# A decoder layer's embedding norm: the weights of the norm spread over the partitions by TensorE, two constant products, and scaling in halves

## The chip, the cores and the metric

The kernel runs on one core of a Trainium2 chip. The metric is the device time in microseconds (us) of one execution; lower is better. Engines are named as in the profile: PE is TensorE (matmul), PEld its weight loads, DVE VectorE, ACT ScalarE, POOL GpSimd, SP SyncE. DMAs are issued from the queues of SP, ACT and POOL. L442 is line 442 of the kernel before.

## The reference, cut to what matters

The reference is one inference step of a hybrid decoder layer (differential attention and gated DeltaNet side by side, then a gated ConvFFN) for a prompt of 512 tokens and 8 sample groups of 8 tokens, with 16 learned meta tokens. The change lies in the layer's first step, which normalises the input and multiplies it with the input projection:

```python
def rmsnorm(x, w):
    xf = x.astype(jnp.float32)
    y = xf * lax.rsqrt(jnp.mean(xf * xf, axis=-1, keepdims=True) + RMS_EPS)
    return (y * w.astype(jnp.float32)).astype(x.dtype)
...
    xn = rmsnorm(x, p['ln_mix_pre'])
    h = xn @ p['w_in']
```

`x` has 512 + 64 + 16 rows of 1024, `ln_mix_pre` is one row of 1024 weights, and `w_in` is 1024 x 5640, all float32.

## The kernel before, in words

`embed` loads the input as five tiles `x` of up to 128 tokens (on partitions) by 1024 channels: four of the prompt, one of 80 rows with the sample and meta tokens. It also loads the first two weight tiles of `w_in` (128 columns each, as two chunks `wraw` of 256 KB) and the norm's weights `lnb`. Every token needs the same 1024 weights, so `lnb` is a tile of 128 x 1024 whose partitions all hold the same row: one DMA on SP's queue, issued between tiles 0 and 1, reads the row 128 times (L428).

`norm(i)` scales tile i. ACT squares the tile and sums each row into `ss` (L439); `rsqrt` makes r from it, with a step on DVE (L374) and a power on POOL (L375); DVE then writes `xs` = x times r times `lnb` (L442), 1024 elements in one instruction. `xs` is a ring of three buffers.

`put(i)` transposes the scaled tile on PE, in two groups of four blocks of 128 x 128 (L411), each group into one PSUM bank `ps_t` (a ring of three). Each group is split into two float32r parts: ACT casts it to `xhi`, and DVE subtracts that from the original to get `xlo` (both in `split`, L305 and L306). Weights are split in the same way into `whi` and `wlo`; for the first weight tile POOL does the subtraction, for the others DVE.

`product(i)` multiplies weight tile i with the columns of tiles 0 and 1: 24 matmuls (hi by hi, hi by lo, lo by hi for eight blocks of 128 channels, L263) into a bank `ps_d`, a ring of two, from which ACT copies the result (`qT`, L1112). The columns of tiles 2 to 4 are multiplied after the embedding. All later projections use the same `xhi` and `xlo`.

Within `embed` each of PE, ACT, DVE and POOL runs its instructions in the order in which the code lists them (`manual_schedule`). That order is: norm 0, norm 1, put 0, the first weights' split, put 1, norm 2, product 0, norm 3, the second weights' split, put 2, norm 4, product 1, put 3, put 4. DMAs on SP's queue keep their own order; each waits for one of eight semaphores to come free, and a load of weights also for a buffer (three `wraw`). After the embedding, instructions of all engines are ordered by a scheduler.

Of the kernel before, what the change touches and what calls it, by code (L numbers as in the profile page):

```python
# [13 lines left out]
ALU = mybir.AluOpType  # L14
# [3 lines left out]
D = 1024  # L18
# [131 lines left out]
class Body:  # L150
# [263 lines left out]
    def embed(self, pool):  # L414
        nc, a = self.nc, self.a
        lnb = self.t(pool, [128, D], "lnb", bufs=1)
        xs = []
        for i in range(5):
            rows = 128 if i < 4 else NTL
            x = self.t(pool, [128, D], "x", bufs=5)  # L420
            if i < 4:
                nc.sync.dma_start(x, a["x_prompt"][0, 128 * i : 128 * i + 128])
            else:
                nc.sync.dma_start(x[0:64], a["x_sample"].rearrange("b t d -> (b t) d"))
                nc.sync.dma_start(x[64:66], a["meta_tokens"][14:16])
                nc.sync.dma_start(x[66:80], a["meta_tokens"][0:14])
            if i == 0:
                nc.sync.dma_start(lnb, a["ln_mix_pre"][0].partition_broadcast(128))  # L428
            xs.append((x, rows))
            if i == 1:  # L430
                raws = [self.raw_w(a["w_in"][0], C_Q)]
        raws.append(self.raw_w(a["w_in"][0], C_Q + 128))

        def norm(i):
            x, rows = xs[i]
            y[i] = self.t(pool, [128, D], "xs", bufs=3)
            junk = self.t(pool, [128, D], "junk", bufs=1)
            ss = self.t(self.small, [128, 1], "ss", bufs=4)
            nc.scalar.activation(junk[:rows], x[:rows], AF.Square, accum_out=ss[:rows])  # L439
            r = self.t(self.small, [128, 1], "r", bufs=4)  # L440
            self.rsqrt(r[:rows], ss[:rows], 1.0 / D, EPS, rows, 1)
            nc.vector.scalar_tensor_tensor(  # L442
                out=y[i][:rows], in0=x[:rows], scalar=r[:rows], in1=lnb[:rows], op0=ALU.mult, op1=ALU.mult
            )

        engines = {mybir.EngineType.PE, mybir.EngineType.Activation, mybir.EngineType.DVE, mybir.EngineType.Pool}
        y, w, first = {}, [], []

        def put(i):
            rows = xs[i][1]  # L450
            self.to_transposed(y[i], rows, *self.part(self.x, (128 * i, 128 * i + rows)))

        def product(i):
            first.append((w[i], self.dense(w[i], self.x, HALF_Q[:1])))

        with self.tc.manual_schedule(engines=engines):
            norm(0)
            norm(1)
            put(0)
            w.append(self.split_w(raws[0], eng=nc.gpsimd))  # L460
            put(1)
            norm(2)
            product(0)
            norm(3)
            w.append(self.split_w(raws[1]))
            put(2)
            norm(4)
            product(1)
            put(3)
            put(4)  # L470
        return first
# [1337 lines left out]
```

## Time and profile before

| what | value |
|---|---|
| median of 3 runs | 1219.9 us (1218.33 to 1222.36) |
| the profiled execution | 1219.77 us, its span 1218.0 us |
| granted TensorE clock, mean | 0.991 |
| PE busy | 1159.3 us, 95% |
| DVE, ACT, POOL busy | 638.2, 447.3 and 206.5 us |
| PE busy from 0 to 25 us | 13.81 us |
| PE busy from 30 to 60 us | 30.00 us |

A row of the timeline gives start and duration in us, engine, line, operation, the tile written and the tile read, shapes, and how many instructions it merges; in brackets stand the engine's idle time before it and what ended it. A row of the chain of waits gives start, duration, engine, tile and line. A row of the DMA answer gives destination and source, queue, count, KB of each, and the median us from issue to landing.

### The profile page before, as it was taken

The page shows a single profiled execution, that of the slowest core. Times are in us where ns is not written, and L with a number is a line of the kernel's source. Part 1 is how long each engine was busy: PE and PEld are TensorE (multiplying, and loading weights), DVE is VectorE, ACT ScalarE, POOL GpSimd, SP SyncE. Part 2 cuts the span into 40 slices and gives each one's busy share as a digit, 9 for nine tenths or more (in the row PEclk, how much of TensorE's full clock was granted, in tenths as well). Part 3 has the DMA queues.
Part 4 walks back from the last instruction along what each step waited for, and adds up shares of the span by engine and source line. Part 5 has one row for each costly group of instructions (what it writes and reads, how often), then busy time and mean ns, then how long its engine had stood idle before and what let it go on. Part 6 is the DMA issues. An engine that isn't in the chain of part 4 may idle for free.

```text
span 1218.0 us, 23729 instructions
## 1 busy us (share of the span) xinstructions
PE 1159.3 (95%) x8927; PEld 1036.0 (85%) x8927; DVE 638.2 (52%) x1719; ACT 447.3 (37%) x1139; POOL 206.5 (17%) x341
## 2 busy tenths in 40 slices
PE   6999999979999989899999999999999999999996
PEld 5977787757687677599998987899999999999996
DVE  5456667596487388346235753455545545422224
ACT  5234445443343243343233433433333333323322
POOL 2122221150241231221010002321111111100000
PEclk9999999999999999999999999999999999999999
DMA  6364525736936946713221552322223223352222
GB/s 197 77 237 133 160 64 180 238 113 201 302 108 192 300 154 192 252 47 86 69 70 55 149 163 87 102 81 85 75 86 88 84 75 88 95 166 79 79 80 85
DMA packets 185002, 157.57 MB, mean 129 GB/s; under 512 B 13234, under 2 KB 147315, under 8 KB 184867
## 3 DMA queue, kind: packets, MB, share of 16 engines
q1 hardware_dynamic: 179569, 147.53, 40.1%
q0 software_dynamic: 4288, 5.16, 1.5%
q10 hardware_dynamic: 1030, 3.35, 0.9%
q8 instruction: 71, 1.16, 0.4%
q14 instruction: 44, 0.36, 0.1%
HBM read 146.12 MB, written 9.88 MB: 128 GB/s over the span
## 4 chain that ended last, share of the span: by engine, by line
PE 69%; issue 13%; DVE 9%; POOL 3%; ACT 3%; DMA 2%; SPq 0%; DVEq 0%; ACTq 0%; POOLq 0%
PE ps_d L263 28%; PE ps_g L263 14%; PE ps_t L263 11%; PE ps_s L263 9%; PE ps_t L411 6%; DVE cy L639 1%; PE ps_m L263 1%; DVE KT L1393 1%; DMA page<-in_cache_k 1%; DMA page<-in_cache_v 1%; DVE vt L646 1%; DVE wlo L306 0%; DVE yn L1744 0%; POOL xr L406 0%; ACT whi L305 0%
## 5 line engine op out<-in xcount | busy, mean ns | idle before, releaser
L306 DVE TENSOR_TENSOR wlo<-wraw,whi 128x512 fp32r<-128x512 f32 x238 | 159.6, 684 | 243.6 <-ACT whi L305 241.9
L305 ACT CAST whi<-wraw 128x512 fp32r<-128x512 f32 x240 | 142.7, 613 | 253.9 <-PE ps_d L263 106.6
L263 PE MATMUL ps_d<-xhi,whi 128*128 128x256 f32 (+2 forms) x704 | 219.0, 311 | 0.0
L263 PE MATMUL ps_d<-xhi,wlo 128*128 128x256 f32 (+2 forms) x704 | 213.5, 304 | 1.2 <-DVE wlo L306 1.2
L263 PE MATMUL ps_d<-xlo,whi 128*128 128x256 f32 (+2 forms) x704 | 213.3, 303 | 0.3 <-DVE xlo L306 0.2
L263 PEld LDWEIGHTS ps_d<-xhi,whi 128*128 128x128 f32 x704 | 134.3, 191 | 7.4 <-issue 4.2
L263 PEld LDWEIGHTS ps_d<-xlo,whi 128*128 128x128 f32 x704 | 134.1, 190 | 3.6 <-issue 2.5
L263 PEld LDWEIGHTS ps_d<-xhi,wlo 128*128 128x128 f32 x704 | 133.8, 190 | 2.6 <-DVE wlo L306 1.6
L411 PE MATMUL ps_t<-consts,page 128*128 128x128 f32 x512 | 73.5, 283 | 8.9 <-DVE KT L1393 7.5
L411 PEld LDWEIGHTS ps_t<-consts,page 128*128 128x128 f32 x512 | 57.5, 143 | 25.5 <-issue 10.3
L263 PE MATMUL ps_t<-fhi,whi 128*128 128x320 f32 (+2 forms) x208 | 62.1, 299 | 0.1
L1393 ACT COPY KT<-ps_t 128x512 f32<-128x512 f32 x64 | 37.4, 585 | 65.5 <-PE ps_t L411 62.8
L263 PE MATMUL ps_t<-flo,whi 128*128 128x320 f32 (+2 forms) x208 | 61.3, 295 | 0.0
L263 PE MATMUL ps_t<-fhi,wlo 128*128 128x320 f32 (+2 forms) x208 | 61.1, 295 | 0.0
L263 PE MATMUL ps_g<-fhi,whi 128*128 128x320 f32 (+2 forms) x200 | 59.5, 298 | 0.0
L263 PE MATMUL ps_g<-flo,whi 128*128 128x320 f32 (+2 forms) x200 | 58.9, 295 | 0.0
L263 PE MATMUL ps_g<-fhi,wlo 128*128 128x320 f32 (+2 forms) x200 | 58.7, 294 | 0.0
L263 PE MATMUL ps_d<-fhi,whi 128*128 128x320 f32 (+2 forms) x192 | 57.4, 299 | 0.2 <-ACT fhi L305 0.2
L263 PE MATMUL ps_d<-flo,whi 128*128 128x320 f32 (+2 forms) x192 | 56.8, 296 | 0.0
L263 PE MATMUL ps_d<-fhi,wlo 128*128 128x320 f32 (+2 forms) x192 | 56.7, 296 | 0.0
L1393 DVE COPY KT<-ps_t 128x512 f32<-128x512 f32 x64 | 43.7, 685 | 18.1 <-PE ps_t L411 17.9
L263 PEld LDWEIGHTS ps_t<-fhi,whi 128*128 128x128 f32 x208 | 39.1, 188 | 0.7 <-ACT whi L305 0.3
(554 smaller groups left out, 2824.6 us busy)
## 6 DMA issues: line engine op xcount, KB each, us to landing
page<-in_cache_k SPq DMA_DIRECT2D x128, 256.0 KB, 4.1
page<-in_cache_v SPq DMA_DIRECT2D x128, 256.0 KB, 4.3
wraw<-in_w_in SPq DMA_DIRECT2D x88, 256.0 KB, 3.4
wraw<-in_w_ffn_in SPq DMA_DIRECT2D x88, 256.0 KB, 3.1
wraw<-in_w_down SPq DMA_DIRECT2D x40, 256.0 KB, 3.0
wraw<-in_w_out SPq DMA_DIRECT2D x16, 256.0 KB, 3.0
x<-in_x_prompt SPq DMA_DIRECT2D x4, 512.0 KB, 7.4
st<-in_state_gdn SPq DMA_DIRECT2D x4, 512.0 KB, 4.1
```

The costliest lines, as they stand in the source:

```text
L263: self.nc.tensor.matmul(out, lhsT, rhs, **kw)
L305: self.nc.scalar.copy(hi, raw)
L306: (eng or self.nc.vector).tensor_tensor(out=lo, in0=raw, in1=hi.bitcast(F32), op=ALU.subtract)
L411: self.nc.tensor.transpose(out, in_, self.ident[:k, :k])
L639: nc.vector.scalar_tensor_tensor(out=y, in0=pre[:, j : j + n], scalar=self.cw[:, ch, 24 + j : 25 + j], in1=y, op0=ALU.mult, op1=ALU.add)
L646: nc.vector.scalar_tensor_tensor(out=dst, in0=part(th), scalar=1.0, in1=part(y_), op0=ALU.add, op1=ALU.mult)
L1393: (nc.scalar.copy if j % 2 else nc.vector.tensor_copy)(kt[:, :, 128 * j : 128 * j + 128], tp)
```

## The change

Three things, all in `embed`:

- The weights come as one row of 4 KB (`lnrow`, one partition), by a DMA on ACT's queue behind the 64 KB of the identity. TensorE multiplies a column of 128 ones with each half of that row, which leaves the weights on all 128 partitions of two PSUM banks (`ps_d`, called `lnp` in the code). Norms 0 and 1 read them there. Two ACT copies then fill `lnb` in SBUF for norms 2 to 4. The broadcast DMA on SP's queue goes.
- DVE fills a tile `warm` of 128 x 512 with ones, and `heat()` multiplies it with itself, once ahead of the two products above and once behind them. The result, in the bank `ps_s`, is not used.
- The scaling of each tile is two instructions of 512 elements in place of one of 1024.

```diff
         lnb = self.t(pool, [128, D], "lnb", bufs=1)
+        row = self.t(pool, [1, D], "lnrow", bufs=1)
+        nc.scalar.dma_start(row, a["ln_mix_pre"])
+        ones = self.t(pool, [1, 128], "ones1", bufs=1)
+        nc.vector.memset(ones, 1.0)
+        warm = self.t(pool, [128, 512], "warm", bufs=1)
+        nc.vector.memset(warm, 1.0)
...
-            if i == 0:
-                nc.sync.dma_start(lnb, a["ln_mix_pre"][0].partition_broadcast(128))
...
-            nc.vector.scalar_tensor_tensor(
-                out=y[i][:rows], in0=x[:rows], scalar=r[:rows], in1=lnb[:rows], op0=ALU.mult, op1=ALU.mult
-            )
+            for g in range(2):
+                sl = slice(512 * g, 512 * g + 512)
+                nc.vector.scalar_tensor_tensor(
+                    out=y[i][:rows, sl], in0=x[:rows, sl], scalar=r[:rows], in1=lnp[g] if i < 2 else lnb[:rows, sl],
+                    op0=ALU.mult, op1=ALU.mult,
+                )
+
+        def heat():
+
+            self.nc.tensor.matmul(self.ps("s"), warm[:, :128], warm, start=True, stop=True)
...
         with self.tc.manual_schedule(engines=engines):
+            heat()
+            lnp = [self.ps("d") for _ in range(2)]
+            for g in range(2):
+                self.nc.tensor.matmul(lnp[g], ones, row[:, 512 * g : 512 * g + 512], start=True, stop=True)
+            heat()
             norm(0)
             norm(1)
+            for g in range(2):
+                nc.scalar.copy(lnb[:, 512 * g : 512 * g + 512], lnp[g])
             put(0)
```

The two places at which the order changes most are ACT's and DVE's work on tiles 0 and 1. In the rows, x_98 and x_104 are tiles 1 and 2 before, x_101, x_103 and x_109 tiles 0, 1 and 2 after; ps_d_125 and ps_d_126 are the two banks with the weights; ps_t are the banks of the transposes; brackets name the engine or DMA whose signal is waited for. ACT before, from tile 1's square to tile 2's:

```order
L439 ACTIVATE junk_127,ss_128<-x_98 128x1024 [waits DMAHW3_49,Activation_49]
L305 CAST xhi_7_87<-ps_t_134 128x4x128 [waits PE_49]
L305 CAST xhi_7_87<-ps_t_141 128x4x128 [waits PE_49]
L305 CAST whi_148<-wraw_100 128x512 [waits DMAHW4_49]
L305 CAST whi_148<-wraw_102 128x512 [waits DMAHW5_49]
L305 CAST xhi_7_87<-ps_t_155 128x4x128 [waits PE_49]
L305 CAST xhi_7_87<-ps_t_162 128x4x128 [waits PE_49]
L439 ACTIVATE junk_170,ss_171<-x_104 128x1024 [waits DMAHW6_49,Activation_49]
```

and now:

```order
L443 ACTIVATE junk_141,ss_142<-x_103 128x1024 [waits DMAHW3_49,Activation_49]
L476 COPY lnb_94<-ps_d_125 128x512 [waits DVE_49]
L476 COPY lnb_94<-ps_d_126 128x512 [waits DVE_49]
L305 CAST xhi_7_87<-ps_t_151 128x4x128 [waits PE_49]
L305 CAST xhi_7_87<-ps_t_158 128x4x128 [waits PE_49]
L305 CAST whi_165<-wraw_105 128x512 [waits DMAHW4_49]
L305 CAST whi_165<-wraw_107 128x512 [waits DMAHW5_49]
L305 CAST xhi_7_87<-ps_t_172 128x4x128 [waits PE_49]
L305 CAST xhi_7_87<-ps_t_179 128x4x128 [waits PE_49]
L443 ACTIVATE junk_187,ss_188<-x_109 128x1024 [waits DMAHW6_49,Activation_49]
```

The two copies are new; they stand ahead of the six casts and wait for a signal of DVE: the first for tile 1's first scaled half, the second for its second half. DVE before, on tiles 0 and 1:

```order
L374 TENSOR_SCALAR r_122<-ss_120 128x1 [waits Activation_49]
L442 SCALAR_TENSOR_TENSOR xs_118<-x_95,r_122,lnb_94 128x1024 [waits DMAHW2_49,DMAHW1_49,Pool_49]
L374 TENSOR_SCALAR r_130<-ss_128 128x1 [waits Activation_49]
L442 SCALAR_TENSOR_TENSOR xs_126<-x_98,r_130,lnb_94 128x1024 [waits DMAHW3_49,Pool_49]
L306 TENSOR_TENSOR xlo_8_88<-ps_t_134,xhi_7_87 128x4x128 [waits Activation_49]
```

and now:

```order
L374 TENSOR_SCALAR r_135<-ss_133 128x1 [waits Activation_49]
L448 SCALAR_TENSOR_TENSOR xs_131<-x_101,r_135,ps_d_125 128x512 [waits DMAHW1_49,PE_49,Pool_49]
L448 SCALAR_TENSOR_TENSOR xs_131<-x_101,r_135,ps_d_126 128x512 [waits PE_49]
L374 TENSOR_SCALAR r_144<-ss_142 128x1 [waits Activation_49]
L448 SCALAR_TENSOR_TENSOR xs_140<-x_103,r_144,ps_d_125 128x512 [waits DMAHW3_49,Pool_49]
L448 SCALAR_TENSOR_TENSOR xs_140<-x_103,r_144,ps_d_126 128x512
L306 TENSOR_TENSOR xlo_8_88<-ps_t_151,xhi_7_87 128x4x128 [waits Activation_49]
```

Each scaling became two, and those of tile 0 wait for PE, which makes the weights, where they waited for the broadcast's landing. On PE the four new products stand ahead of tile 0's transposes. On SP's queue the load of the rest of the constants (`consts`, 885.5 KB) moved ahead of the fourth weight chunk; on ACT the fourth chunk's cast moved behind the copy `qT` of product 0. From there on all engines have the same order as before.

## The prediction

> **What bounds the kernel now.** I read the page first, then the chain of waits for the first 60 us, and then each engine's rows in order of time for the start, where the whole change lies.
>
> ```profile
> PE 1159.3 (95%) x8927; PEld 1036.0 (85%) x8927; DVE 638.2 (52%) x1719; ACT 447.3 (37%) x1139; POOL 206.5 (17%) x341
> ```
>
> Over the span TensorE is the bound. The chain (start, us, what) shows from when:
>
> ```profile
> 9.37 0.57 POOL r L375
> 9.96 1.30 DVE xs L442
> 11.30 1.13 PE ps_t L411 x4
> 12.45 0.59 ACT xhi L305
> 13.07 0.70 DVE xlo L306
> ...
> 25.45 26.37 PE ps_d L263 x190
> ```
>
> From 25.45 on, PE runs 26 us with no wait. Before that it waits in turn for DVE and ACT: the norms, the transposes' evacuations and the splits. So the change is worth what it moves the point 25.45. ACT's rows there:
>
> ```profile
> 4.70 1.06 ACT L439 ACTIVATE junk<-x 128x1024 f32<-128x1024 f32 x1 [2.19 <-DMA x<-in_x_prompt]
> 7.95 1.06 ACT L439 ACTIVATE junk<-x 128x1024 f32<-128x1024 f32 x1 [2.10 <-DMA x<-in_x_prompt]
> 9.22 0.59 ACT L305 CAST xhi<-ps_t 128x512 fp32r<-128x512 f32 x1
> 10.07 0.59 ACT L305 CAST xhi<-ps_t 128x512 fp32r<-128x512 f32 x1 [0.27 <-PE ps_t L411]
> 10.56 1.14 ACT L305 CAST whi<-wraw 128x512 fp32r<-128x512 f32 x2
> 12.45 0.59 ACT L305 CAST xhi<-ps_t 128x512 fp32r<-128x512 f32 x1 [0.75 <-PE ps_t L411]
> 13.30 0.59 ACT L305 CAST xhi<-ps_t 128x512 fp32r<-128x512 f32 x1 [0.27 <-PE ps_t L411]
> 13.79 1.06 ACT L439 ACTIVATE junk<-x 128x1024 f32<-128x1024 f32 x1
> 17.89 1.07 ACT L305 CAST xhi<-ps_t 128x512 fp32r<-128x512 f32 x2 [0.20 <-PE ps_t L411]
> ```
>
> Each `norm` begins with a square. Tile 2's starts at 13.79, right behind six casts for tiles 0 and 1, and everything to 25.45 hangs on it: r, the scaling, the splits, one after another on DVE. I follow the change to this one point, 13.79.
>
> **The change, part by part.** *The 512 KB broadcast goes from SP's queue.* Nobody waited for it; the tile's answer says so, since each scaling waited for r:
>
> ```profile
> its engine sat idle before it (us, times) until:
>   POOL r L375: 3.4, 5
> ```
> ```profile
> x<-in_x_prompt SPq DMA_DIRECT2D x4, 512.0 KB, 7.4
> lnb<-in_ln_mix_pre SPq DMA_DIRECT2D x1, 512.0 KB
> wraw<-in_w_in SPq DMA_DIRECT2D x88, 256.0 KB, 3.4
> ```
> ```profile
> 19.01 1.28 DVE L306 TENSOR_TENSOR wlo<-wraw,whi 128x512 fp32r<-128x512 f32 x2
> ```
> ```profile
> 11.25 2.51 POOL L306 TENSOR_TENSOR wlo<-wraw,whi 128x512 fp32r<-128x512 f32 x2 [1.33 <-ACT whi L305]
> ```
>
> The tiles are as large as the broadcast, and tiles 0 and 1 are there at 4.70 and 7.95 with it between them: two transfers take 3.25, so tile 1 lands near 6.3 and its square ends near 7.5 instead of 9.1. SP keeps its order but for the large `consts` load, which now goes ahead of the fourth weight chunk. That chunk waits for a buffer until POOL has split the first one, which ACT casts near 13.4: 13.4 + 1.25, and 3.4 to land, is 18.1. DVE splits it from 19.01 before, so not ahead of 20 now if the sum below holds. I cost it at nothing; without this cover it would be a few tenths.
>
> *The row.* It leaves ACT's queue behind the identity's 64 KB and is under way while the tiles load:
>
> ```profile
> 0.77 0.42 ACTq L198 DMA_DIRECT2D consts<-in_constants  x1
> consts<-in_constants ACTq DMA_DIRECT2D x1, 64.0 KB, 4.1
> x<-in_x_sample SPq DMA_DIRECT2D x1, 256.0 KB, 9.4
> out_new_ffn_conv_prompt<-ftailT POOLq DMA_DIRECT2D x22, 1.0 KB, 1.6
> ```
>
> The identity lands at 0.77 + 4.1 = 4.9. The row is issued at 1.2. Bounds: 1.2 + 1.6 = 2.8 as a small transfer on idle queues, 1.2 + 9.4 = 10.6 as the worst that was queued in this stretch. I take 4.9, the nearest row: same queue, same moment, directly behind it.
>
> *Four products of 512 columns in f32.* Two records make one product:
>
> ```profile
> 244.60 1.02 PE L263 MATMUL ps_g<-dd,consts 128*128 128x512 f32 x2
> 8.07 1.97 PE L411 MATMUL ps_t<-consts,xs 128*128 128x128 f32 x8 [8.07 <-DVE xs L442]
> 17.22 1.07 PE L411 MATMUL ps_t<-consts,xs 128*128 128x128 f32 x8
> 14.62 0.41 PE L263 MATMUL ps_d<-xlo,whi 128*128 128x256 f32 x1
> 14.83 0.32 PE L263 MATMUL ps_d<-xhi,wlo 128*128 128x256 f32 x1
> 14.99 0.28 PE L263 MATMUL ps_d<-xhi,whi 128*128 128x256 f32 x1
> 15.11 0.28 PE L263 MATMUL ps_d<-xlo,whi 128*128 128x256 f32 x1
> ```
> ```profile
> 1.91 0.53 POOL L1107 MEMSET vt<- 64x512 f32 x1
> ```
>
> At 244.60 a product takes 0.86 of PE plus 0.2 until its result. The same eight transposes take 1.97 early and 1.07 late, and products follow each other at 0.21 until 14.83 and at 0.12 after it: PE starts at half pace. So a product costs 1.7 there. The first constant product, after a fill on DVE that I take at POOL's 0.53, runs from about 1.6 to 3.3, under PE's idle time before 8.07: nothing. The two that spread the weights end, with results, at 4.9 + 1.7 + 0.2 = 6.8 and 8.5, and the second constant product ends near 10.1, ahead of tile 0's transposes. At half pace the four groups of transposes then end near 11.1, 12.0, 12.9 and 14.3; ACT's casts of them, below, come later each time, so this product costs nothing either. With ACT free it would cost up to 1.7.
>
> *Scaling in halves from PSUM.* DVE's rows:
>
> ```profile
> 6.73 1.28 DVE L442 SCALAR_TENSOR_TENSOR xs<-x,r,lnb 128x1024 f32<-128x1024 f32 x1 [0.69 <-POOL r L375]
> 9.13 0.15 DVE L374 TENSOR_SCALAR r<-ss 128x1 f32<-128x1 f32 x1 [1.12 <-ACT junk L439]
> 9.96 1.28 DVE L442 SCALAR_TENSOR_TENSOR xs<-x,r,lnb 128x1024 f32<-128x1024 f32 x1 [0.67 <-POOL r L375]
> 11.16 1.28 DVE L306 TENSOR_TENSOR xlo<-ps_t,xhi 128x512 fp32r<-128x512 f32 x2
> ...
> 13.07 0.69 DVE L306 TENSOR_TENSOR xlo<-ps_t,xhi 128x512 fp32r<-128x512 f32 x1 [0.63 <-ACT xhi L305]
> ```
>
> Two halves that read PSUM take 1.28 together (11.16), as one full scaling does, and one takes 0.69: the split itself is free, in all five norms. But on DVE, as the order above shows, the second half of tile 0 stands ahead of tile 1's first step, and its new wait on PE holds that step. So: tile 0's halves start at 6.9 and 8.6 and end at 9.3; tile 1's step starts at 9.25; from step to scaling takes 9.96 - 9.13 = 0.83; tile 1's halves end at 10.05 + 0.69 = 10.75 and 11.35. Tile 1's earlier arrival is lost here: its square has been done since 7.5.
>
> *The two copies to `lnb`.* In ACT's order above they wait for DVE, not for PE: each for the last scaling that reads its bank, tile 1's first and second half. Behind them stand all six casts and tile 2's square, which before could use ACT's idle time (0.27 + 0.75 + 0.27, and 9.22 on). [...] If they were allowed to go as soon as a weight product is there (7.6 and 8.6), the casts would wait only for the transposes behind the second constant product, and tile 2's square would start between 13.2 (PE at full pace) and 14.4 (at half): about the time of before.
>
> **The sum.** Copies start at 10.8 and 11.4. Casts follow each other at 0.48 (17.89: two in 1.07) or 0.52 (10.56: two in 1.14), and the copies I price alike: 11.4 + 0.48 + 2 x 0.48 + 2 x 0.52 + 2 x 0.48 = 14.84. Before: 13.79. That is 1.05 later. From there to 25.45 the steps are the same and as long; PE has slack in them; then PE is saturated and hands the 1.05 on. The profiled execution took 1219.77 (span 1218.0 and 1.77 around it), beside a median of 1219.9 of the runs shown: 1219.77 + 1.05 = 1220.8. In general the shift is the row's landing less 3.85. Its lower end is where r alone binds: halves from 6.73, tile 1's first half done at 9.46, square at 13.55, 0.25 earlier than before: 1219.5, for any row landed by 3.6. PE's earlier full pace buys nothing that I can see: transposes and the first product wait for ACT, not ACT for them.
>
> **The rivals.** *A, the row lands early.* For it: 1.6 us for 1 KB. Against: 4.1 for the 64 KB ahead of it. It gives 1219.5. [...] Chance 0.14.
>
> *B, the clock and the early tile reach the path.* If the copies' wait is not what ends last and the row is early, ACT can begin the casts near 9 and tile 2's square comes near 11.9: 1.9 earlier, 1217.9. For it: the early transposes cost 0.9 more than later ones, twice, and tile 1 waits 2.1 us for its load. Against: the order above. Chance 0.08. A further 0.03 for more than that.
>
> *C, the row lands late, and it is slower.* A transfer can take 9.4 us in this stretch, as the sample rows did. Then DVE, ACT and all behind them start from 10.6: 10.6 - 3.85 = 6.8 more, 1226.5. It decides beyond a landing at 7.5. Against: those rows stood behind tiles and weights in their own queue, this one behind 64 KB. Chance 0.07; and 0.03 that half pace of PE lasts through the first products and adds over 3 us.
>
> **How the numbers follow.** The forecast, 1220.8, has 0.65; A 0.14, B 0.08 (and 0.03 beyond), C 0.07 (and 0.03). About 0.3% (3.7 us) is what a measurement of this kernel can tell from no change; forecast, A and B lie within it: same 0.87, faster 0.03, slower 0.10. The range reaches down over A and B to 1217.9 and up by a row 2.5 us later than taken, 1223.3; C lies outside.
>
> **What would show it.** In the changed profile: PE's constant product near 1.6, the weight products from about 4.9, tile 0's second half after 8.5, ACT's copies after tile 1's halves (near 10.8 and 11.4), tile 2's square near 14.8, and PE's unbroken stretch from 26.5 instead of 25.45. Copies before 9.5 or that stretch beginning before 25 make the forecast wrong; so does a weight product starting before 4 or after 6.

## The result, and the profile after

The changed kernel takes 1223.47 us (median of 16 runs, 1221.55 to 1226.09) against 1219.07 for the kernel before (16 runs): a ratio of 1.0041, interval 1.0031 to 1.0051. It is slower by 4.4 us, 0.4%, where 1220.8 and "within 0.3%" were forecast. The profiled execution took 1222.98 us, span 1221.2. One run of the kernel before (1285.39 us) and one of a later version (1640.45 us) were slow, at granted clocks of 0.842 and 0.635; all times and ratios leave them out.

On the page PE is busier by 7.4 us. The four new products at half pace (2.07 for one, where one takes 1.02 at 244.60 before) account for it (2.07 + 3.78 + 2.08 = 7.93); they stand ahead of tile 0's transposes, where PE had mostly been idle:

```profile
PE 1166.7 (96%) x8935; PEld 1037.0 (85%) x8935; DVE 638.1 (52%) x1726; ACT 447.5 (37%) x1141; POOL 205.7 (17%) x341
```

The start went nearly as forecast. PE's rows (start, us, what, idle time ahead of it and what ended it):

```profile
1.68 2.07 PE L455 MATMUL ps_s<-warm 128*128 128x512 f32 x2 [1.68 <-DVE gc L590]
4.78 3.78 PE L471 MATMUL ps_d<-lnrow,ones 1*128 1x512 f32 x4 [1.02 <-DMA lnrow<-in_ln_mix_pre]
8.48 2.08 PE L455 MATMUL ps_s<-warm 128*128 128x512 f32 x2
10.35 2.77 PE L411 MATMUL ps_t<-consts,xs 128*128 128x128 f32 x12
```

DVE's and ACT's rows of the same stretch:

```profile
6.96 0.75 DVE L448 SCALAR_TENSOR_TENSOR xs<-x,r,ps_d 128x512 f32<-128x512 f32 x1 [1.25 <-PE ps_d L471]
8.60 0.75 DVE L448 SCALAR_TENSOR_TENSOR xs<-x,r,ps_d 128x512 f32<-128x512 f32 x1 [0.89 <-PE ps_d L471]
10.07 1.41 DVE L448 SCALAR_TENSOR_TENSOR xs<-x,r,ps_d 128x512 f32<-128x512 f32 x2 [0.67 <-POOL r L375]
16.99 1.42 DVE L448 SCALAR_TENSOR_TENSOR xs<-x,r,lnb 128x512 f32<-128x512 f32 x2 [0.67 <-POOL r L375]
```
```profile
6.16 1.06 ACT L443 ACTIVATE junk<-x 128x1024 f32<-128x1024 f32 x1 [0.64 <-DMA x<-in_x_prompt]
10.86 1.24 ACT L476 COPY lnb<-ps_d 128x512 f32<-128x512 f32 x2 [3.55 <-DVE xs L448]
14.95 1.10 ACT L443 ACTIVATE junk<-x 128x1024 f32<-128x1024 f32 x1
```

Tile 1 is there at 6.16, and its square, 1.06 us, is done long before DVE takes it up. The copies start at 10.86, behind DVE, and tile 2's square at 14.95: 1.16 later than before. The chain's unbroken stretch on PE begins at

```profile
26.91 26.48 PE ps_d L263 x190
```

instead of 25.45: 1.46 late. The other 3 us are lost much later. From here on PE has the same instructions in the same order in both kernels. It waits longer at three places, near 694, 739 and 1189. Three rows of before, then those of after:

```profile
690.62 0.38 PE L263 MATMUL ps_g<-bhi,wlo 128*128 128x256 f32 x1 [0.52 <-DVE wlo L306]
739.21 0.72 PE L411 MATMUL ps_t<-consts,y 66*128 66x66 f32 x8 [1.24 <-DVE y L395]
1189.47 0.44 PE L411 MATMUL ps_t<-consts,yT 128*128 128x128 f32 x2 [0.42 <-ACT yT L1722]
```
```profile
690.86 0.39 PE L263 MATMUL ps_g<-bhi,wlo 128*128 128x256 f32 x1 [0.76 <-DVE wlo L306]
694.28 0.38 PE L263 MATMUL ps_s<-ahi,whi 128*128 128x256 f32 x1 [0.18 <-ACT whi L305]
695.48 0.38 PE L263 MATMUL ps_s<-ahi,wlo 128*128 128x256 f32 x1 [0.71 <-DVE wlo L306]
741.28 0.71 PE L411 MATMUL ps_t<-consts,y 66*128 66x66 f32 x8 [1.91 <-DVE y L395]
1192.62 0.44 PE L411 MATMUL ps_t<-consts,yT 128*128 128x128 f32 x2 [1.48 <-ACT yT L1740]
```

That is 0.18 + 0.67 = 0.85 near 694 (before waits 0.04 for the last of these products), 0.67 near 739 and 1.06 near 1189: 2.58, and with the start 4.04, against 4.40 between the medians. The wait at 690 is not counted: it is 0.80 in the version below that changes nothing but the PSUM banks.

The two profiled spans differ by 3.2 only. The rest lies where PE's granted clock falls to half for some 3.41 us, which comes at other places in the two executions: before has such a stretch from 656.60 that after lacks, after has one from 82.05 that before lacks. Waits beside these stretches differ too (after waits 0.79 less near 85 and 1.08 less near 465). So the account by single rows is good to about 1 us (4.04 against 3.2), no better. The windows on the stretch near 656, before and after (us, then busy time and instructions of PE, PEld, DVE, ACT, POOL, then the granted clock):

```profile
656.00:662.00 6.00, 6.00 (x37) 6.00 (x36) 5.94 (x17) 3.88 (x11) 0.00 (x0) 0.72 0.00 0
```
```profile
658.00:664.00 6.00, 6.00 (x47) 5.95 (x45) 6.00 (x17) 3.93 (x11) 0.00 (x0) 1.00 0.00 0
```

Behind all three places stands, directly or a few steps back, a cast on ACT that waits for a weight chunk. Near 739 it is the fifth chunk of `w_out`, cast 6.40 us behind the first, where before took 5.47. ACT's rows at the last place, before and after:

```profile
1186.19 0.43 ACT L1722 COPY yT<-ps_t 128x320 f32<-128x320 f32 x1 [1.61 <-PE ps_t L263]
1188.53 0.62 ACT L305 CAST whi<-wraw 128x512 fp32r<-128x512 f32 x1 [1.92 <-DMA wraw<-in_w_down]
1189.06 0.36 ACT L1722 COPY yT<-ps_t 128x256 f32<-128x256 f32 x1
```
```profile
1188.28 0.43 ACT L1740 COPY yT<-ps_t 128x320 f32<-128x320 f32 x1 [1.61 <-PE ps_t L263]
1191.68 0.62 ACT L305 CAST whi<-wraw 128x512 fp32r<-128x512 f32 x1 [2.98 <-DMA wraw<-in_w_down]
1192.21 0.36 ACT L1740 COPY yT<-ps_t 128x256 f32<-128x256 f32 x1
```

The second copy of yT stands behind a cast that waits for the chunk: 2.34 us from copy to cast before, 3.40 after. What moves on the DMA engines in the 2.3 us from 0.6 ahead of the first copy, by queue and kind (packets, MB, share of 16 engines), before (1185.6 to 1187.9) and after (1187.7 to 1190.0):

```profile
q1 hardware_dynamic: 1050, 0.52, 76.3%
```
```profile
q1 hardware_dynamic: 965, 0.48, 75.8%
q8 instruction: 1, 0.02, 2.6%
```

The page calls the kind of the added line `instruction`; it is read here as a load of program code, an engine's next instructions brought in by DMA. Over the whole span both kernels have as many of them:

```profile
q8 instruction: 71, 1.16, 0.4%
q14 instruction: 44, 0.36, 0.1%
```

Queue 8 carries 16 KB each (1.16 MB / 71). The trace of before has 18125 records of PE (8927 products, 8927 weight loads and 271 of its sequencer), so that is one load for every 255 of them. Queue 14 carries 8 KB each (0.36 MB / 44); by the author's estimate it serves the other four engines, one load for every 127 of their 5604 records. The packet times of the trace put queue 8's load 1.76 us behind yT's copy before, just when the chunk's last packet is in, and 0.52 behind it after, where it takes 0.95 us, as one packet, in the middle of the chunk. So theory 4 below arose: a load of code comes when an engine has run through a fixed count of instructions. In the two traces this holds nearly: queue 8's load at yT's copy starts when 17836 records of PE have begun before and 17833 after, its last one at 18080 and 18081, and queue 14's last one when 2112 of DVE have begun in both. The change adds 17 records on PE (eight products, eight weight loads, one of the sequencer) and 8 on DVE, all in the embedding; by theory 4 every later load comes that much earlier in the program, and some fall on a transfer that PE waits for.

### The profile page after: what moved, and what is told of

It reads as the page before. It is cut to its first block, busy times and chain, and to the rows that moved or that the text cites. A ratio compares the mean times of both kernels' runs of the same rounds, so it can differ in the third digit from the quotient of the medians.

```text
span 1221.2 us, 23756 instructions
## 1 busy us (share of the span) xinstructions
PE 1166.7 (96%) x8935; PEld 1037.0 (85%) x8935; DVE 638.1 (52%) x1726; ACT 447.5 (37%) x1141; POOL 205.7 (17%) x341
## 3 DMA queue, kind: packets, MB, share of 16 engines
q8 instruction: 71, 1.16, 0.4%
## 4 chain that ended last, share of the span: by engine, by line
PE 70%; issue 13%; DVE 9%; ACT 3%; POOL 3%; DMA 1%; DVEq 0%; ACTq 0%; SPq 0%; POOLq 0%
PE ps_d L263 29%; PE ps_g L263 14%; PE ps_t L263 11%; PE ps_s L263 9%; PE ps_t L411 6%; DVE cy L657 1%; PE ps_m L263 1%; DVE KT L1411 1%; DMA page<-in_cache_v 1%; DVE wlo L306 0%; ACT whi L305 0%; POOL r L375 0%; DVE yn L1762 0%; POOL xr L406 0%; POOL hss L375 0%
## 5 line engine op out<-in xcount | busy, mean ns | idle before, releaser
L263 PE MATMUL ps_g<-fhi,wlo 128*128 128x320 f32 (+2 forms) x200 | 58.7, 294 | 0.0
```

The costliest lines, as they stand in the source:

```text
L263: self.nc.tensor.matmul(out, lhsT, rhs, **kw)
```

## The experiments

Theory 1: a delay of the start is passed on, and something else makes the rest. Theory 2: the delay itself makes later waits grow. Theory 3: other PSUM banks. Theory 4: places of the code loads. Theory 5: number of instructions. Times are medians beside the kernel before in the same session; ratios have 95% intervals.

**Only a delay.** Before, and:

```diff
             put(1)
+            scrap = self.t(pool, [128, D], "scrap", bufs=1)
+            nc.scalar.activation(scrap, xs[1][0], AF.Square)
+            nc.scalar.activation(scrap[:, :384], xs[1][0][:, :384], AF.Square)
             norm(2)
```

> The kernel before with nothing changed but two extra squares on ACT (128x1024 and 128x384, into a scrap tile) ahead of tile 2's square, some 1.5 us. Tile 2's square should start near 15.2 instead of 13.79 and PE's unbroken stretch near 26.9 instead of 25.45, as in the changed kernel. Theory 1 (a delay of the start is passed on one to one, and the other 3 us of the change come from something else that it did): 1219.1 + 1.5 = 1220.6. Theory 2 (the later 3 us are a consequence of the delay itself: waits further on grow when the start is late): 1223 to 1224.

Measured: 1221.74 against 1219.52, ratio 1.0010 (0.9999 to 1.0022), that is +1.2 us (-0.1 to +2.7); the medians lie 2.2 apart. Tile 2's square starts at 15.37. 4.4 is outside, and PE's waits at the three places are nearly those of before (0.17, 1.31 and 0.46; cast 2.38 behind the copy), so theory 2 does not explain them. But the version does not show that a delay is passed on one to one. In its trace SP issues some small loads later than before (`al` at 29.56, before at 21.91), and PE's stretch is broken:

```profile
45.28 0.39 PE L263 MATMUL ps_d<-xhi,whi 128*128 128x322 f32 x1 [1.29 <-DVE qm L1126]
```

**Only the banks, both ways.** Before with the tags touched first, and the changed kernel likewise in the other order:

```diff
+            for tag in "sdd":        # in the changed kernel: "tttdds", ahead of heat()
+                self.ps(tag)
             norm(0)
```

> The kernel before with only the PSUM banks renumbered as in the changed kernel (score tag on bank 0, product tag on 1 and 2, transpose tag on 3 to 5, instead of 5, 3 and 4, 0 to 2); no instruction is added. The stretch should still begin at 25.45. Theory 3 (the other banks cost the later 3 us): 1222. Theories 1 and 2: 1219.1, as before.

> The changed kernel with the PSUM banks of the kernel before (transpose tag 0 to 2, product tag 3 and 4, score tag 5). The stretch should begin near 26.9, as in the changed kernel. Theory 3 (banks): 1223.5 - 3 = 1220.5. Theories 1 and 2: 1223.5.

Measured: 1219.15 against 1219.52, ratio 0.9996 (0.9986 to 1.0006); and 1224.28, ratio 1.0038 (1.0025 to 1.0050). Banks cost nothing; theory 3 fell.

**The change without its constant products.** Both `heat()` calls, the function and `warm` go.

> The changed kernel without its two constant products and their filled tile (nothing else). By the steps of the prediction the second half of tile 0 is still what the second weight product allows and the copies wait for tile 1's halves, so the stretch should begin near 26.9 again, or up to 0.3 us later where PE's transposes run longer at half pace. Total 1223.5 by theories 1 to 3 (banks: without them the score tag comes after the others, so 1220.5 to 1223.5 by theory 3); 1220.5 if the constant products themselves, by a changed course of the clock, make the later 3 us.

Measured: 1223.01, ratio 1.0032 (1.0018 to 1.0046). The stretch begins at 26.77. So the constant products, and what they do to the clock, are not the cause. With 10 records more than before on PE, where the changed kernel has 17, the later waits differ: none extra near 739, and more near 1189:

```profile
739.35 0.72 PE L411 MATMUL ps_t<-consts,y 66*128 66x66 f32 x8 [1.23 <-DVE y L395]
1190.99 0.44 PE L411 MATMUL ps_t<-consts,yT 128*128 128x128 f32 x2 [1.79 <-ACT yT L1732]
```

**Before with a few idle instructions more.** One kernel has the DVE part, one the PE part, one both:

```diff
+        scrap = self.t(pool, [128, 1], "scrap", bufs=1)
+        for _ in range(8):
+            nc.vector.memset(scrap, 1.0)
         xs = []
...
+            for tag in "tttdds":
+                self.ps(tag)
+            for _ in range(4):
+                nc.tensor.matmul(self.ps("s")[:32, :32], self.mhalf, self.phalf, start=True, stop=True)
             norm(0)
```

> The kernel before with eight more instructions on DVE and nothing else: eight memsets of one 128x1 scrap tile in the first us, where DVE is idle. Theory 4 (the loads of program code, 8 KB for DVE and 16 KB for PE, come at fixed counts of instructions; a few more instructions at the start move every later load relative to the work, and some then fall on a weight transfer that PE waits for): the point 25.45 stays, but DVE's code loads near 695 and 1191.7 come 5 to 6 us earlier in the program, as in the changed kernel, and the total is 1220 to 1222, the more of it the more of the later 3 us hangs on DVE's loads rather than PE's. Any theory by which only the start counts: 1219.5, as before.

> The kernel before with four more small products on PE at its start (32 columns, f32, into the score tag's bank; PE is idle there until 8.07), so that PE's instructions are as many as in the changed kernel less one; the banks are numbered as before. Theory 4: PE's code load near 1187.95 comes about 1 us earlier, into the transfer that ACT's cast waits for, and the total is 1220 to 1222; with dve8 it shares the later 3 us. Theories by which only the start counts: 1219.5.

> Both together: the kernel before with eight more memsets on DVE and four more small products on PE at its start, nothing else; its norms, broadcast and order are those of before. Theory 4: the start unchanged (25.45), both kinds of code loads where they are in the changed kernel, the cast behind yT's copy some 3.4 to 3.7 us after it instead of 2.34, total 1222 (before 1219.5, and the 2.5 to 3 us of the change that its start does not explain). Theories by which only the start or the clock counts: 1219.5.

Measured, against 1219.15: DVE's alone 1220.65, ratio 1.0015 (1.0000 to 1.0030), at the edge of the noise; PE's alone 1221.85, ratio 1.0024 (1.0009 to 1.0039); both 1223.87, ratio 1.0031 (1.0015 to 1.0046), that is +3.8 us (1.8 to 5.6). The granted clock of the runs differs a little (mean 0.9883 with both, 0.9894 before). Over all runs of these kernels the time grows by some 0.75 us for each 0.001 less, so by this estimate the clock goes with 0.8 of the 3.8. In the chain of the kernel with both, the start is that of before, and PE has the waits of after:

```profile
25.41 26.38 PE ps_d L263 x190
```
```profile
692.49 0.39 PE L263 MATMUL ps_s<-ahi,wlo 128*128 128x256 f32 x1 [0.69 <-DVE wlo L306]
738.32 0.71 PE L411 MATMUL ps_t<-consts,y 66*128 66x66 f32 x8 [1.97 <-DVE y L395]
1190.39 0.44 PE L411 MATMUL ps_t<-consts,yT 128*128 128x128 f32 x2 [1.53 <-ACT yT L1729]
```

With DVE's eight alone, the wait near 694 is there and the other two are as before; with PE's four alone, it is the other way round (0.13 near 694):

```profile
692.74 0.39 PE L263 MATMUL ps_s<-ahi,wlo 128*128 128x256 f32 x1 [0.45 <-DVE wlo L306]
737.96 0.71 PE L411 MATMUL ps_t<-consts,y 66*128 66x66 f32 x8 [1.24 <-DVE y L395]
1188.35 0.44 PE L411 MATMUL ps_t<-consts,yT 128*128 128x128 f32 x2 [0.55 <-ACT yT L1725]
```
```profile
741.16 1.14 PE L411 MATMUL ps_t<-consts,y 66*128 66x66 f32 x8 [2.36 <-DVE y L395]
1196.25 0.44 PE L411 MATMUL ps_t<-consts,yT 128*128 128x128 f32 x2 [1.69 <-ACT yT L1726]
```

So what DVE adds costs near 694, what PE adds near 739 and 1189.

**Before with a whole load of idle instructions more.** The same, with 128 memsets over 16 scrap tiles (24 of them behind `norm(0)`) and 64 products of one column that accumulate: 256 records on PE.

> The kernel before with 128 more memsets on DVE (104 ahead of its first step, 24 between tile 0's scaling and tile 1's) and 64 more one-column products on PE at its start (256 records on PE): one whole code load more for each, so that all later loads fall at the same places of the program as before. Theory 4 (what counts is where the loads fall): 1219.5, as before, plus whatever the start shows in its trace (0 to 2 us where the pads are not done in time), with the load behind yT's copy at +1.8 and the cast at +2.3 to +2.4. Theory 5 (more instructions at the start cost time in themselves, by their number): at least the 4 us of the kernel with eight memsets and four products, 1223.5 or more.

Measured: 1219.14 against 1219.51, ratio 0.9996 (0.9984 to 1.0009). This decides between theories 4 and 5: sixteen times as many extra instructions cost nothing that was measured, and PE's load at the last chunk is back where it fell before. The window on that chunk has no code load again (it comes 1.84 us behind the copy, 1.76 before), and the waits are those of before:

```profile
q1 hardware_dynamic: 1022, 0.51, 75.2%
```
```profile
737.82 0.71 PE L411 MATMUL ps_t<-consts,y 66*128 66x66 f32 x8 [1.24 <-DVE y L395]
1188.27 0.44 PE L411 MATMUL ps_t<-consts,yT 128*128 128x128 f32 x2 [0.57 <-ACT yT L1732]
```

**The same inside the changed kernel.** Nothing of the change is taken out; 120 memsets (80 at the start, 16 between tile 0's halves, 24 ahead of `put(0)`) and 60 one-column products (14, 20 and 26 of them ahead of the first `heat()`, behind it and behind `put(1)`) fill its additions up to a whole load.

> The changed kernel, all its parts kept, with 120 more memsets on DVE and 60 more one-column products on PE in its first 15 us, so that the change's own additions and these make one whole code load more for each engine (DVE 8 + 120 = 128 instructions, PE 17 + 240 = 257 records). Theory 4: the loads fall where they do in the kernel before, the cast behind yT's copy at +2.3 to +2.5 instead of +3.4, no lost time near 694, 739 and 1189; the total is before plus what its start shows (1.46 of the changed kernel and what the pads add in the trace): 1219.5 + 1.5 = 1221 with the pads hidden, 1223.5 - 2.5 for short. Theory 5 (the number of instructions), or another cause of the later loss in the change itself: 1223.5 or more.

Measured: 1221.65 against 1219.62, ratio 1.0014 (1.0001 to 1.0026), +1.7 us (0.1 to 3.2). Tile 2's square is at 15.27 and the stretch begins at 27.23, 1.78 late, and nothing is lost at the three places: the cast is 2.47 behind yT's copy, and PE waits 0.00, 1.24 and 0.55 there. So what the change loses beyond its start is the place of the code loads.

**The row first.** The changed kernel with as many instructions, but the identity's DMA behind the row's:

```diff
-        nc.scalar.dma_start(self.ident, self.a["constants"][:, 0:128])
...
         nc.scalar.dma_start(row, a["ln_mix_pre"])
+        nc.scalar.dma_start(self.ident, a["constants"][:, 0:128])
```

> The changed kernel with the row's DMA issued ahead of the identity's on ACT's queue; as many instructions on every engine as in the changed kernel. The row should land by 2.8 as in the version with one wide PSUM tile (2.3), the weight products end by 6.6, tile 0's halves start at 6.9 and 7.6, the copies near 9.3 and 10, tile 2's square near 13.5 (14.95 in the changed kernel), the stretch near 25.5 (26.91). Theory 4 (the start is passed on one to one, code loads as in the changed kernel): 1223.5 - 1.4 = 1222.1, still slower than before. If all of the change's loss were its start: 1219.5.

Measured: 1222.86 against 1219.51, ratio 1.0030 (1.0018 to 1.0041). The products follow the constant product at once and the square is at 13.86:

```profile
3.69 3.78 PE L471 MATMUL ps_d<-lnrow,ones 1*128 1x512 f32 x4
9.77 1.24 ACT L476 COPY lnb<-ps_d 128x512 f32<-128x512 f32 x2 [2.58 <-DVE xs L448]
13.86 1.10 ACT L443 ACTIVATE junk<-x 128x1024 f32<-128x1024 f32 x1
```

The stretch begins at 25.82, 0.37 later than before, and yet the kernel is 3.6 us slower than before. Nearly all of that is the later loss.

**The copies later.** The changed kernel with the two copies in `norm(2)`, behind the square:

> The changed kernel with the two copies to lnb behind tile 2's square on ACT instead of ahead of tile 0's casts; as many instructions but for one wait. The casts then wait for the transposes only: tile 0's transposes end near 12 (second constant product until 10.4), tile 2's square near 14 instead of 14.95, the copies beside r's steps on DVE and POOL; the stretch near 26. Theory 4: 1223.5 - 0.9 = 1222.6. If the copies' wait is not what moves the start, the stretch stays at 26.9.

Measured: 1224.32, ratio 1.0046 (1.0031 to 1.0060). This expectation missed. The square comes at 14.44, but the copies then stand ahead of tile 3's square and delay tile 2's scaling, and the stretch begins at 27.32, 0.4 later than with the copies in front. Their time (1.24 in front, 1.08 here) is ACT's wherever they stand.

**A quicker start, and the same with its loads put back.** Row first, one PSUM tile of two banks that all five norms read in one full scaling, no copies, no halves, no constant products; the second adds 62 one-column products on PE (24 ahead of the weight products, 38 behind):

```diff
+            lnp = self.t(psum_l, [128, 2, 512], "ps_l", bufs=1)
             for g in range(2):
+                self.nc.tensor.matmul(lnp[:, g], ones, row[:, 512 * g : 512 * g + 512], start=True, stop=True)
...
+                out=y[i][:rows], in0=x[:rows], scalar=r[:rows], in1=lnp.rearrange("p g c -> p (g c)")[:rows],
```

> A version of the change meant to be quicker at the start with code counts near those of before (DVE one fewer, PE three more, ACT one more): the row's DMA goes ahead of the identity on ACT's queue, the two weight products write one PSUM tile of two banks that all five norms read in one full scaling (no copies to lnb, no halves), no constant products, the ones on POOL. If the row's landing was set by the 64 KB ahead of it, it lands near 3.3; the scaling of tile 0 starts near 7, tile 1's near 9, tile 2's square between 11.9 and 13.5 instead of 13.79, PE's stretch 0.3 to 1.9 earlier than 25.45. Total 1217.5 to 1219.2 by theory 4 if its loads stay clear of the transfers; PE's loads are moved by three, so up to 1.5 more where those count.

> The version with the row first, one wide PSUM tile, no copies, no halves and no constant products, with 62 one-column products on PE ahead of and behind the weight products (248 records and the 9 of the change: one code load), DVE as it was (one fewer than before). Without them it lost its 1.1 us of the start and 3 us behind yT's copy near 1189.5 and came out at 1218.75, like before. Theory 4: that loss goes, and the start keeps 0.5 to 1.5 us of its gain (PE also is at full pace sooner, since the products keep it busy): 1216 to 1218.5 against 1219.5. If the loss at 1189.5 has another cause: 1218.8 or more.

Measured: 1218.75 against 1219.15, ratio 1.0000 (0.9985 to 1.0015); with the loads put back 1218.59 against 1219.62, ratio 0.9984 (0.9972 to 0.9996), by the ratio 1.9 us faster than before (0.5 to 3.4), by the medians 1.0. The first gains 1.1 us at its start and loses it where PE waits 1.97 for yT. In the second the stretch begins 1.33 earlier than before, and that wait is short:

```profile
24.12 26.58 PE ps_d L262 x190
```
```profile
1189.71 0.44 PE L410 MATMUL ps_t<-consts,yT 128*128 128x128 f32 x2 [0.55 <-ACT yT L1736]
```

It is the only version of these runs whose interval lies below the kernel before.

**All versions beside each other.** The packet times of the fifteen traces agree on the place at 1189. In eight of them PE's code load starts 0.48 to 1.53 us behind yT's copy, and the cast comes 3.40 to 3.89 behind it: the changed kernel, that with the old banks, that without constant products, the two with four products on PE, the row first, the copies later and the quicker start. In the other seven the load starts 1.69 to 1.93 behind the copy, and the cast comes at 2.34 to 2.50.

With the quicker start the load lasts from 1.53 to 2.62; by 1.76, 1053 of the 1056 packets of the chunk's queue have ended, and the last three end at 2.75, behind the load; the cast comes at 3.89.

Near 739, PE's load starts 2.36 to 3.67 us behind the first cast of `w_out` in six versions, where PE then waits 1.68 to 2.36, and 4.69 to 8.23 behind it in the other nine, where it waits 1.23 to 1.52. Near 694, 7 instructions more on DVE (without constant products; the copies later) leave no wait, 8 leave 0.45 to 0.71.

## Why the prediction was wrong

**The start, right.** The row landed by 4.78 (4.9 forecast), the weight products went through from there, the first constant product cost nothing, the halves of tile 0 began at 6.96 and 8.60 (6.9 and 8.6), the copies began at 10.86 (10.8), and tile 2's square at 14.95 (14.84). That the shift follows the row's landing is shown: with the row first, the square came 1.09 earlier (13.86; 13.55 was the bound given for an early row).

**"The split itself is free", wrong by a little.** Two halves took 1.41, not the 1.28 of one full scaling. Before the square that hardly shows. Behind it DVE scales tiles 2 and 3 in one chain: it is 1.20 late at tile 2's scaling (16.99 against 15.79), 1.32 at tile 3's and 1.45 at the weight split behind that, and no later after it. These 2 x 0.13 = 0.26 and the square, 0.11 later and 0.04 longer than summed, take the stretch from 26.5 to 26.9. The prediction had priced the halves from another instruction's pair.

**"Then PE is saturated and hands the 1.05 on", the step that failed.** The second half of the step fits the runs, within wide intervals: with the loads in place, a start 1.78 late cost 1.7 (0.1 to 3.2), and one 1.33 early gained 1.9 (0.5 to 3.4). But PE is not saturated. Of the 58.7 us that it idles before (1218.0 - 1159.3), 11.2 lie ahead of 25 us (25 - 13.81) and 47.5 behind, and there it still waits, for weight chunks among others. The step took for granted that equal instructions behind 25.45 would take equal time. They did not: 2.58 us more waiting at three places, 0.85 near 694 with DVE's code loads and 1.73 near 739 and 1189 with PE's. The sum had no term for what a few instructions at the start do to the whole program, and the range, built from the start alone, ended at 1223.3.

**The rivals.** A: the row did not land early behind 64 KB. Alone at the head of its queue it did: issued at 0.75 in the version with the quicker start, it was used by a product at 2.30. So the row took 1.55 at most there, and 3.6 (1.21 to 4.78) behind the identity. B: PE's early full pace bought nothing, as argued; the kernel without constant products started its stretch at 26.77, with them at 26.91. C: the row was not late. The slower side came from a mechanism that no rival named.

PE's and DVE's loads differ in these runs: 16 KB for PE, one per some 255 records, and, by the estimate above, 8 KB on queue 14 for DVE. With 256 records more on PE and 128 instructions more on DVE at once, PE waited at the three places as before (none near 694, then 1.24 and 0.57).

What stays open: every version was profiled in one execution, and how much one load costs was seen to vary (PE's wait near 1189 grew by 1.06 to 1.55 us). Near 694 and 739 the chain from the load to the chunk was not followed packet by packet, and no run moved a load without adding instructions.

## What to carry to other kernels

In this kernel PE waits for weight chunks with little slack, and some 0.3% hung on where the loads of program code fell: eight memsets and four small products at the start cost 3.8 us (1.8 to 5.6), and the quicker start lost there the 1.1 us that it had gained. When a kernel changes by a few us and its edited stretch does not explain it, line up the same instructions of both traces and look at the first waits that differ, with the instruction queues of those windows beside them. To judge an edit by itself, fill its instructions up to a whole load (here 256 records on PE, 128 instructions on DVE) and compare then.

## What the hardware showed that was not expected

Loads of program code moved on the DMA engines beside the data: 71 of 16 KB and 44 of 8 KB in this kernel, 0.4% and 0.1% of the engines' time by the page. While PE's load ran from 1188.80 to 1189.75 after, two of the last chunk's packets took 0.58 and 0.60 us, where their median is 0.027 and the longest of before 0.119. By their place alone the loads were worth some 3 us (0.25%), by an estimate from the 3.8 of the kernel with both less the 0.8 of the clock. Eight memsets and four small products on idle engines in the first 3 us made the kernel 3.8 us slower (1.8 to 5.6); 128 and 64 of them changed nothing that could be measured (ratio 0.9996, 0.9984 to 1.0009).
